# Column sums of a 32768 x 2048 matrix: the last 8-row load shared by two engines, and a first load of 8 rows for each of 48 partitions

## The chip, the cores and the metric

The kernel runs on one core of a Trainium2 chip. The metric is the time of one execution on the device, in microseconds (us). The median of three runs of the kernel before is 628.78 us (628.78 to 629.19). A separate execution was taken with the hardware profiler; every duration below comes from it.

The core has a matrix engine (TensorE, in the profile PE), a vector engine (VectorE, DVE), a scalar engine (ScalarE, ACT), GpSimd (POOL) and SyncE (SP), which here only issues transfers. 16 DMA engines move data between the chip's memory (HBM) and the on-chip memory (SBUF), which has 128 partitions. TensorE writes its sums to PSUM.

## What is computed

```python
def setup_inputs():
    batch, seq, dim = 32, 1024, 2048
    return {
        "grad_output": np.random.randn(batch, seq, dim).astype(np.float32),
    }

def reference(grad_output: np.ndarray) -> np.ndarray:
    return np.sum(grad_output, axis=(0, 1)).astype(np.float32)
```

The input is 32768 rows of 2048 float32 values, 268 MB; the output is one row of 2048 sums. The order of the rows does not matter.

## The kernel before, in words

The matrix is read as a flat list of 32768 rows, that is 256 rows for each of 128 partitions. A load of "m rows" takes 128 x m neighbouring rows and gives each partition m of them, which are contiguous in HBM, so that one partition's piece is m x 8 KB. All loads are issued by SP, in the order of the list `loads`, each with the semaphore that it waits for before it is issued (`after`) and the one that it raises by 16 on landing (`lane`).

The SBUF tile `ring` has three slots (`SLOTS`) of 8 rows (`TILE`) for each partition. The loads, in order:

- `head`, 1 row, into a tile of its own (L84)
- 30 blocks of 8 rows, block k into slot k mod 3 (L85 to L87). From block 3 on, load k waits until the semaphore `vec` has reached k-2, which is the first VectorE add of block k-2. That add is the last reader of the slot which block k overwrites.
- 5 rows into slot 0 (L90), after the first add of block 28; 4 rows into slot 1 (L92), after that of block 29; four loads of 1 row (L93, L94), each after TensorE has used the row which it overwrites (`used`)
- the last two rows, each cut into a left part of 1536 columns and a right part of 512, first both left parts, then both right parts (L99 to L105)

VectorE reduces each block. The first add of block k adds the 4 rows (`WIDE`) left by block k-1 to the first 4 rows of block k, and raises `vec`; the second adds rows 4 to 7 of the block to rows 0 to 3 (L143 to L146, in a loop of 9 passes of 3 blocks). `settle()` drains VectorE between adds that depend on each other. Blocks 28 and 29 and the load of 4 rows are folded to one row by smaller adds, which are ordered by a semaphore `step` (L150 to L173).

TensorE sums over the partitions. A matmul with a column of ones adds one row of each partition into PSUM; the 2048 columns are cut into six pieces, four in LEFT (1536 columns) and two in RIGHT (512), and each piece is two matmul instructions. So a row costs 12. It takes the 5 rows, the four rows loaded one by one, the row that VectorE leaves, and the two last rows in halves (L197 to L209). In the loop of the single rows it also runs filler matmuls of 256 columns whose result nobody reads (L202).

At the end ScalarE and VectorE copy the sums from PSUM to SBUF, left columns first (L219 to L224), and SP writes them out in two transfers (L225 to L228).

Of the kernel before, what the change touches and what calls it, by code (L numbers as in the profile page):

```python
# [8 lines left out]
P = 128  # L9
# [4 lines left out]

SLOTS = 3
TILE = 8
TILES = 30
WIDE = 4
LANES = 4
SMALL = 4  # L20
LAST = 2


LOOPS = 9
ROUNDS = 2

FILLER = 256

LEFT = ((0, 416, 0), (416, 416, 1), (832, 352, 2), (1184, 352, 3))
RIGHT = ((1536, 256, 2), (1792, 256, 3))  # L30
# [3 lines left out]
def kernel(  # L34
# [5 lines left out]
    nc = tc.nc  # L40
    fp32 = mybir.dt.float32
    D = out.shape[-1]
    flat = grad_output.rearrange("b s d -> (b s) d")
    R = flat.shape[0]
    assert (1 + TILE * TILES + 1 + LANES * ROUNDS + SMALL + LAST) * P == R
    assert TILES == SLOTS * (LOOPS + 1)

    const_pool = ctx.enter_context(tc.tile_pool(name="const", bufs=1))
    psum_pool = ctx.enter_context(tc.tile_pool(name="psum", bufs=1, space=bass.MemoryType.PSUM))

    ring = const_pool.tile([P, SLOTS * TILE * D], fp32)
    head = const_pool.tile([P, D], fp32)
    ones = const_pool.tile([P, 1], fp32)
    warm = const_pool.tile([1, 1], fp32)
    psum = psum_pool.tile([P, 3 * 512], fp32)

    names = ("one", "zero", "vec", "step", "used", "mm_left", "mm_right", "done")  # L60
    one, zero, vec, step, used, mm_left, mm_right, done = (tc.alloc_semaphore(n) for n in names)
    slot_in = [tc.alloc_semaphore(f"slot{s}") for s in range(SLOTS)]
    row_in = [tc.alloc_semaphore(f"row{j}") for j in range(LANES)]
    rows_in, small_in = tc.alloc_semaphore("rows"), tc.alloc_semaphore("small")
    last_in = [tc.alloc_semaphore(f"last{i}") for i in range(2 * LAST)]
    left = [tc.alloc_semaphore(f"left{i}") for i in range(2)]
    right = [tc.alloc_semaphore(f"right{i}") for i in range(2)]
    head_in = tc.alloc_semaphore("head")

    def rows(at, m):  # L70
        return ring[:, at * D : (at + m) * D]

    at_row = 0
    loads = []

    def load(m, dst, lane, after=None, first=None, lo=0, hi=D):
        nonlocal at_row
        if first is None:
            first = at_row
            at_row += P * m  # L80
        src = flat[first : first + P * m].rearrange("(p m) d -> p m d", p=P)[:, :, lo:hi]
        loads.append((dst.rearrange("p (m d) -> p m d", m=m), src, lane, after))

    load(1, head[:], head_in)  # L84
    for k in range(TILES):  # L85
        s = k % SLOTS
        load(TILE, rows(s * TILE, TILE), slot_in[s], (vec, k - 2) if k >= SLOTS else None)  # L87


    load(1 + LANES, rows(0, 1 + LANES), rows_in, (vec, TILES - 2))  # L90
    small_at = TILE
    load(SMALL, rows(small_at, SMALL), small_in, (vec, TILES - 1))  # L92
    for j in range(LANES):  # L93
        load(1, rows(j, 1), row_in[j], (used, j + 1))  # L94
    at = (small_at + SMALL) * D
    res_at = at + LAST * D
    final = []
    cut = RIGHT[0][0]
    for lo, hi, pieces in ((0, cut, LEFT), (cut, D, RIGHT)):  # L99
        for j in range(LAST):  # L100
            n = hi - lo
            lane = last_in[len(final)]
            load(1, ring[:, at : at + n], lane, (vec, TILES - 1), at_row + j * P, lo, hi)
            final.append((at, lo, pieces, lane, j == LAST - 1))
            at += n  # L105

# [6 lines left out]
    def take(engine, lane):  # L113
        engine.wait_ge(lane, 16).then_inc(lane, -16)  # L114

    def settle():
        nc.vector.drain(fusable=False)

    def vadd(at, other, n):
        return nc.vector.tensor_add(out=rows(at, n), in0=rows(at, n), in1=other)  # L120

    section = tc.tile_critical(no_gpsimd_drain=True)
    section.__enter__()  # L123
# [2 lines left out]

    nc.gpsimd.memset(ones[:], 1.0).then_inc(one, 1)  # L127

    for lane in row_in:
        nc.gpsimd.wait_ge(rows_in, 16).then_inc(lane, 16)  # L130


    nc.vector.memset(psum[:, : 2 * 512], 0.0).then_inc(zero, 1)  # L133
    take(nc.vector, slot_in[0])
    vadd(0, rows(WIDE, WIDE), WIDE)
    nc.vector.wait_ge(head_in, 16)
    settle()
    vadd(0, head[:], 1)
    with nc.vector.Fori(0, LOOPS):
        for s in (1, 2, 0):  # L140
            at, before = s * TILE, (s - 1) % SLOTS * TILE
            take(nc.vector, slot_in[s])
            settle()  # L143
            vadd(at, rows(before, WIDE), WIDE).then_inc(vec, 1)
            settle()
            vadd(at, rows(at + WIDE, WIDE), WIDE)  # L146
    n_step = 0
    settle()

    def fold(at, height, to, after=None):  # L150
        nonlocal n_step
        while height > to:
            n = min(height // 2, height - to)
            height -= n
            add = vadd(at, rows(at + height, n), n).then_inc(step, 1)
            if after is not None:
                add._wait_ge(*after)
            n_step += 1
            after = (step, n_step)

    height = WIDE
    for k, to in ((TILES - 2, 2), (TILES - 1, 1)):
        at, before = k % SLOTS * TILE, (k - 1) % SLOTS * TILE
        take(nc.vector, slot_in[k % SLOTS])
        add = vadd(at, rows(before, height), height).then_inc(vec, 1)
        if n_step:
            add._wait_ge(step, n_step)
        fold(at, TILE, to, (vec, k))
        height = to
    nc.vector.wait_ge(small_in, 16)  # L170
    fold(small_at, SMALL, 1)
    vadd(at, rows(small_at, 1), 1)._wait_ge(step, n_step).then_inc(step, 1)
    n_step += 1  # L173

# [5 lines left out]
    def matmuls(at, pieces, base=0, wait=None, start=False, then=None):  # L182
        for lo, n, g in pieces:
            x = at + lo - base
            mat = nc.tensor.matmul(  # L185
                sums[lo], lhsT=ones[:], rhs=ring[:, x : x + n], start=start, stop=then is not None
            )
            if wait is not None:
                mat._wait_ge(*wait)
                wait = None  # L190
            if then is not None:
                mat.then_inc(then, 1)
        return mat

    nc.tensor.wait_ge(one, 1)
    nc.tensor.wait_ge(zero, 1)
    matmuls(LANES * D, LEFT + RIGHT, wait=(rows_in, 16), start=True)  # L197
    with nc.tensor.Fori(0, ROUNDS):
        for j, lane in enumerate(row_in):
            take(nc.tensor, lane)  # L200
            if FILLER:
                nc.tensor.matmul(  # L202
                    psum[96:97, 2 * 512 : 2 * 512 + FILLER], lhsT=ones[:], rhs=rows(j, 1)[:, :FILLER], start=True, stop=True
                )
            matmuls(j * D, LEFT + RIGHT).then_inc(used, 1)
    matmuls(at * D, LEFT + RIGHT, wait=(step, n_step))
    for x, lo, pieces, lane, stop in final:
        then = (mm_left if pieces is LEFT else mm_right) if stop else None
        matmuls(x, pieces, lo, wait=(lane, 16), then=then)  # L209


    nc.scalar.copy(out=warm[:], in_=ones[0:1, :])._wait_ge(one, 1)  # L212
# [6 lines left out]
    for copy, half in ((nc.scalar.copy, 0), (nc.vector.tensor_copy, 1)):  # L219
        for i in range(2):  # L220
            lo, n, _ = LEFT[2 * half + i]
            result(copy, lo, n, (mm_left, len(LEFT)), left[half])
        lo, n, _ = RIGHT[half]
# [39 lines left out]
```

## Time and profile before

| Quantity | Before |
|---|---|
| median of 3 runs | 628.78 us |
| the profiled execution | 628.72 us |
| its span (first to last instruction of the program) | 626.9 us |
| VectorE busy | 533.2 us (85%) |
| TensorE busy (matmuls) | 18.8 us (3%) |
| idle time of VectorE ahead of its adds | 84.8 us |
| idle time of TensorE ahead of its first matmul | 598.5 us |
| granted TensorE clock | 0.999 |

A start or an end in the timeline is counted from the beginning of the span. "Idle before" of a group is the time in which the engine did nothing just before its instructions, and the name behind the arrow is what ended most of it: "DVEq L114" is VectorE's own queue standing at the wait of L114 for a block to land. A DMA's time counts from its issue to its landing, so that a transfer which queues behind another seems long. The line of the adds is always L120, that of the helper `vadd`, and that of the matmuls L185.

### The profile page before, as it was taken

To read this page: it belongs to the slowest core of one execution; us is meant where nothing else is said; L and a number is where in the kernel's file an instruction comes from. 1 tells how busy PE (TensorE), PEld (TensorE's weight loads), DVE (VectorE), ACT (ScalarE), POOL (GpSimd) and SP (SyncE) were. 2 spreads that over 40 slices of the span, in tenths; PEclk is the share of its full clock that TensorE was granted. 3 is DMA by queue.
4 is the path that set the end of the run, shared out by engine and by line. 5 is a ranking of instruction groups with operands and counts; after the bars stand their busy time and mean duration, and the time that the engine had idled before them with its cause. 6 is when DMAs were issued, how large, how long until landed. Compare 5 with 4: busy or idle time off the path is not lost. (4 is left out here: it accounts for less than half of the span.)

```text
span 626.9 us, 628 instructions
## 1 busy us (share of the span) xinstructions
PE 18.8 (3%) x160; PEld 6.9 (1%) x160; DVE 533.2 (85%) x70; ACT 2.8 (0%) x5; POOL 0.3 (0%) x5
## 2 busy tenths in 40 slices
PE   0000000000000000000000000000000000000056
PEld 0000000000000000000000000000000000000022
DVE  0349988889888898888988889988889888898995
ACT  0000000000000000000000000000000000000000
POOL 0000000000000000000000000000000000000000
PEclk9999999999999999999999999999999999999999
DMA  9999999999999999999999999999999999999997
GB/s 401 401 468 401 468 401 468 401 468 401 468 401 464 406 456 414 447 422 427 443 427 443 422 447 410 460 406 464 401 468 401 468 401 468 401 468 401 427 415 297
DMA packets 5909, 268.46 MB, mean 428 GB/s; under 512 B 658, under 2 KB 658, under 8 KB 1172
## 3 DMA queue, kind: packets, MB, share of 16 engines
q1 hardware_dynamic: 5908, 268.45, 99.1%
q8 instruction: 1, 0.02, 0.0%
HBM read 268.44 MB, written 0.01 MB: 428 GB/s over the span
## 5 line engine op out<-in xcount | busy, mean ns | idle before, releaser
L120 DVE TENSOR_TENSOR ring<-ring 128x8192 f32<-128x8192 f32 (+2 forms) x65 | 528.6, 8134 | 84.8 <-DVEq L114 82.0
L185 PE MATMUL psum<-ring,ones 128*1 128x352 f32 (+2 forms) x144 | 18.8, 496 | 598.9 <-DMA ring<-in_grad_output_dram 598.9
L185 PEld LDWEIGHTS psum<-ring,ones 128*1 128x1 f32 x144 | 6.5, 86 | 607.6 <-DMA ring<-in_grad_output_dram 600.7
L216 DVE COPY ring<-psum 1x352 f32<-1x352 f32 (+1 forms) x3 | 1.4, 486 | 5.1 <-PE psum L185 5.0
L202 PE MATMUL psum<-ring,ones 128*1 128x256 f32 x16 | 5.2, 410 | 6.1 <-PEq L114 6.1
L216 ACT COPY ring<-psum 1x416 f32<-1x416 f32 (+1 forms) x3 | 1.4, 453 | 620.6 <-PE psum L185 620.5
L120 DVE TENSOR_TENSOR ring<-ring,head 128x2048 f32<-128x2048 f32 x1 | 2.3, 2293 | 0.1
L133 DVE MEMSET psum<- 128x1024 f32 x1 | 0.9, 912 | 1.2 <-SPq L123 1.2
L202 PEld LDWEIGHTS psum<-ring,ones 128*1 128x1 f32 x16 | 1.2, 88 | 8.7 <-issue 8.0
L212 ACT ACT_TABLE_LOAD x1 | 1.3, 1283 | 0.9 <-SPq L123 0.9
L212 ACT COPY warm<-ones 1x1 f32<-1x1 f32 x1 | 0.2, 190 | 0.0
L247 POOL MEMSET const-bfloat16-1.0<- 128x1 bf16 x1 | 0.1, 102 | 0.0
L247 POOL MEMSET const-uint8-127<- 128x1 uint8 x1 | 0.1, 102 | 0.0
L127 POOL MEMSET ones<- 128x1 f32 x1 | 0.1, 100 | 0.5 <-SPq L123 0.5
L247 POOL MEMSET const-float32-0.0<- 128x1 f32 x1 | 0.1, 99 | 0.2 <-issue 0.2
L247 POOL MEMSET const-float32-1.0<- 128x1 f32 x1 | 0.1, 99 | 0.0
## 6 DMA issues: line engine op xcount, KB each, us to landing
ring<-in_grad_output_dram SPq DMA_DIRECT2D x1, 5120.0 KB, 22.6
ring<-in_grad_output_dram SPq DMA_DIRECT2D x1, 4096.0 KB, 14.7
ring<-in_grad_output_dram SPq DMA_DIRECT2D x4, 1024.0 KB, 9.2
ring<-in_grad_output_dram SPq DMA_DIRECT2D x2, 768.0 KB, 13.0
head<-in_grad_output_dram SPq DMA_DIRECT2D x1, 1024.0 KB, 4.9
ring<-in_grad_output_dram SPq DMA_DIRECT2D x2, 256.0 KB, 14.0
ring<-in_grad_output_dram SPq DMA_DIRECT2D x30, 29.8
out_dram<-ring SPq DMA_DIRECT2D x1, 6.0 KB
```

The costliest lines, as they stand in the source:

```text
L120: return nc.vector.tensor_add(out=rows(at, n), in0=rows(at, n), in1=other)
L127: nc.gpsimd.memset(ones[:], 1.0).then_inc(one, 1)
L133: nc.vector.memset(psum[:, : 2 * 512], 0.0).then_inc(zero, 1)
L185: mat = nc.tensor.matmul(sums[lo], lhsT=ones[:], rhs=ring[:, x : x + n], start=start, stop=then is not None)
L202: nc.tensor.matmul(psum[96:97, 2 * 512 : 2 * 512 + FILLER], lhsT=ones[:], rhs=rows(j, 1)[:, :FILLER], start=True, stop=True)
L212: nc.scalar.copy(out=warm[:], in_=ones[0:1, :])._wait_ge(one, 1)
L216: copy(out=res[:, lo : lo + n], in_=sums[lo])._wait_ge(*wait).then_inc(then, 1)
L247: nc = _bacc.Bacc("TRN2", target_bir_lowering=False, num_devices=1)
```

## The change

- `WIDE` goes from 4 to 2. VectorE's part of a block becomes three adds: 2 rows of the block before into this block, then 4 rows, then 2 rows. `vec` is raised by the first of them, as before.
- The first load is no longer 1 row for each of 128 partitions, but 8 rows for each of 48 partitions (`FEW`), the partitions 0 to 47, into slot 2 of the ring. VectorE folds it to 2 rows on 48 partitions and adds these to block 0. Load 2, which overwrites slot 2, now waits for that add. `vec` is one higher than before for the same block, and the gates stand at k-1 instead of k-2.
- The loads of 5, 4 and four times 1 row are gone. In their place come a load of 8 rows into slot 0 (`share_in`), and loads of 2 and 1 rows (`REST`); the last two rows are split as before.
- Of the shared load TensorE takes rows 0 to 2 directly (`DIRECT`). VectorE adds rows 3 to 7 and the sum of everything before (row 8) into row 3, first the left 1536 columns, then the right 512, and raises `sum_left` and `sum_right`. TensorE takes the left sum ahead of the first left part, and the right sum after it, ahead of the second left part.
- The filler matmuls, their loop on TensorE, GpSimd's four waits and the semaphores of the single rows go.

The core of the diff:

```diff
-WIDE = 4
-LANES = 4
-SMALL = 4
+FEW = 48
+WIDE = 2
+DIRECT = 3
+REST = (2, 1)
...
-    load(1, head[:], head_in)
+    head_at = 2 * TILE
+    load(TILE, rows(head_at, TILE)[:FEW], head_in, parts=FEW)
     for k in range(TILES):
         s = k % SLOTS
-        load(TILE, rows(s * TILE, TILE), slot_in[s], (vec, k - 2) if k >= SLOTS else None)
-
-
-    load(1 + LANES, rows(0, 1 + LANES), rows_in, (vec, TILES - 2))
-    small_at = TILE
-    load(SMALL, rows(small_at, SMALL), small_in, (vec, TILES - 1))
-    for j in range(LANES):
-        load(1, rows(j, 1), row_in[j], (used, j + 1))
-    at = (small_at + SMALL) * D
+        load(TILE, rows(s * TILE, TILE), slot_in[s], (vec, k - 1) if k >= 2 else None)
+
+    load(TILE, rows(0, TILE), share_in, (vec, TILES - 1))
+    sum_at = TILE
+    at = sum_at + 1
+    rest = []
+    for m, lane in zip(REST, rest_in):
+        load(m, rows(at, m), lane, (vec, TILES))
+        rest.append((at, m, lane))
+        at += m
+    at *= D
...
-            load(1, ring[:, at : at + n], lane, (vec, TILES - 1), at_row + j * P, lo, hi)
+            load(1, ring[:, at : at + n], lane, (vec, TILES), at_row + j * P, lo, hi)
...
+    nc.vector.wait_ge(head_in, 16)
+    fold(head_at, TILE, WIDE, FEW)
     take(nc.vector, slot_in[0])
-    vadd(0, rows(WIDE, WIDE), WIDE)
-    nc.vector.wait_ge(head_in, 16)
-    settle()
-    vadd(0, head[:], 1)
+    add = vadd(0, rows(head_at, WIDE), WIDE, parts=FEW).then_inc(vec, 1)
+    add._wait_ge(step, n_step)
+    nc.vector.wait_ge(vec, 1)
+    fold(0, TILE, WIDE)
+    nc.vector.wait_ge(step, n_step)
     with nc.vector.Fori(0, LOOPS):
         for s in (1, 2, 0):
             at, before = s * TILE, (s - 1) % SLOTS * TILE
             take(nc.vector, slot_in[s])
             settle()
             vadd(at, rows(before, WIDE), WIDE).then_inc(vec, 1)
-            settle()
-            vadd(at, rows(at + WIDE, WIDE), WIDE)
+            n = TILE
+            while n > WIDE:
+                n //= 2
+                settle()
+                vadd(at, rows(at + n, n), n)
...
+    nc.vector.wait_ge(share_in, 16)
+    for lo, hi, ready in ((0, cut, sum_left), (cut, D, sum_right)):
+        n = TILE - DIRECT + 1
+        while n > 1:
+            m = n // 2
+            x = grid[:, DIRECT : DIRECT + m, lo:hi]
+            add = nc.vector.tensor_add(out=x, in0=x, in1=grid[:, DIRECT + n - m : DIRECT + n, lo:hi])
+            n -= m
+            add._wait_ge(step, n_step)
+            if n > 1:
+                add.then_inc(step, 1)
+                n_step += 1
+            else:
+                add.then_inc(ready, 1)
...
-    matmuls(LANES * D, LEFT + RIGHT, wait=(rows_in, 16), start=True)
-    with nc.tensor.Fori(0, ROUNDS):
-        for j, lane in enumerate(row_in):
-            take(nc.tensor, lane)
-            if FILLER:
-                nc.tensor.matmul(
-                    psum[96:97, 2 * 512 : 2 * 512 + FILLER], lhsT=ones[:], rhs=rows(j, 1)[:, :FILLER], start=True, stop=True
-                )
-            matmuls(j * D, LEFT + RIGHT).then_inc(used, 1)
-    matmuls(at * D, LEFT + RIGHT, wait=(step, n_step))
-    for x, lo, pieces, lane, stop in final:
+    for i in range(DIRECT):
+        matmuls(i * D, LEFT + RIGHT, wait=None if i else (share_in, 16), start=i == 0)
+    for at, m, lane in rest:
+        for i in range(m):
+            matmuls((at + i) * D, LEFT + RIGHT, wait=None if i else (lane, 16))
+    matmuls(DIRECT * D, LEFT, wait=(sum_left, 1))
+    for i, (x, lo, pieces, lane, stop) in enumerate(final):
         then = (mm_left if pieces is LEFT else mm_right) if stop else None
         matmuls(x, pieces, lo, wait=(lane, 16), then=then)
+        if i == 0:
+            matmuls(DIRECT * D, RIGHT, wait=(sum_right, 1))
```

More of the change, by code (lines that the diff above doesn't have):

```diff
@@ L16 @@
 TILE = 8
+FEW = 48
 TILES = 30
-WIDE = 4
-LANES = 4
-SMALL = 4
+WIDE = 2
+DIRECT = 3
+REST = (2, 1)
 LAST = 2
 LOOPS = 9
-ROUNDS = 2
-FILLER = 256
 LEFT = ((0, 416, 0), (416, 416, 1), (832, 352, 2), (1184, 352, 3))
@@ L44 @@
     R = flat.shape[0]
-    assert (1 + TILE * TILES + 1 + LANES * ROUNDS + SMALL + LAST) * P == R
+    assert FEW * TILE + (TILE * TILES + TILE + sum(REST) + LAST) * P == R
     assert TILES == SLOTS * (LOOPS + 1)
@@ L51 @@
     ring = const_pool.tile([P, SLOTS * TILE * D], fp32)
-    head = const_pool.tile([P, D], fp32)
     ones = const_pool.tile([P, 1], fp32)
     warm = const_pool.tile([1, 1], fp32)
[L55 to L65, printed above, removed]
+    psum = psum_pool.tile([P, 2 * 512], fp32)
+    names = ("one", "zero", "vec", "step", "sum_left", "sum_right", "mm_left", "mm_right", "done")
+    one, zero, vec, step, sum_left, sum_right, mm_left, mm_right, done = (tc.alloc_semaphore(n) for n in names)
     left = [tc.alloc_semaphore(f"left{i}") for i in range(2)]
     right = [tc.alloc_semaphore(f"right{i}") for i in range(2)]
-    head_in = tc.alloc_semaphore("head")
+    head_in, share_in = tc.alloc_semaphore("head"), tc.alloc_semaphore("share")
+    slot_in = [tc.alloc_semaphore(f"slot{s}") for s in range(SLOTS)]
+    rest_in = [tc.alloc_semaphore(f"rest{i}") for i in range(len(REST))]
+    last_in = [tc.alloc_semaphore(f"last{i}") for i in range(2 * LAST)]
+    grid = ring.rearrange("p (m d) -> p m d", d=D)
     def rows(at, m):
@@ L74, with load @@
     loads = []
-    def load(m, dst, lane, after=None, first=None, lo=0, hi=D):
+    def load(m, dst, lane, after=None, first=None, lo=0, hi=D, parts=P):
         nonlocal at_row
@@ L79, in load @@
             first = at_row
-            at_row += P * m
-        src = flat[first : first + P * m].rearrange("(p m) d -> p m d", p=P)[:, :, lo:hi]
+            at_row += parts * m
+        src = flat[first : first + parts * m].rearrange("(p m) d -> p m d", p=parts)[:, :, lo:hi]
         loads.append((dst.rearrange("p (m d) -> p m d", m=m), src, lane, after))
-    load(1, head[:], head_in)
+    head_at = 2 * TILE
+    load(TILE, rows(head_at, TILE)[:FEW], head_in, parts=FEW)
     for k in range(TILES):
         s = k % SLOTS
-        load(TILE, rows(s * TILE, TILE), slot_in[s], (vec, k - 2) if k >= SLOTS else None)
-    load(1 + LANES, rows(0, 1 + LANES), rows_in, (vec, TILES - 2))
-    small_at = TILE
-    load(SMALL, rows(small_at, SMALL), small_in, (vec, TILES - 1))
-    for j in range(LANES):
-        load(1, rows(j, 1), row_in[j], (used, j + 1))
-    at = (small_at + SMALL) * D
+        load(TILE, rows(s * TILE, TILE), slot_in[s], (vec, k - 1) if k >= 2 else None)
[8 more added lines that the diff above has]
+    at *= D
     res_at = at + LAST * D
@@ L117, in settle, with vadd @@
         nc.vector.drain(fusable=False)
-    def vadd(at, other, n):
-        return nc.vector.tensor_add(out=rows(at, n), in0=rows(at, n), in1=other)
+    def vadd(at, other, n, to=None, parts=P):
+        out = rows(at if to is None else to, n)
+        return nc.vector.tensor_add(out=out[:parts], in0=rows(at, n)[:parts], in1=other[:parts])
     section = tc.tile_critical(no_gpsimd_drain=True)
@@ L127, with stepped, fold @@
     nc.gpsimd.memset(ones[:], 1.0).then_inc(one, 1)
-    for lane in row_in:
-        nc.gpsimd.wait_ge(rows_in, 16).then_inc(lane, 16)
-    nc.vector.memset(psum[:, : 2 * 512], 0.0).then_inc(zero, 1)
-    take(nc.vector, slot_in[0])
-    vadd(0, rows(WIDE, WIDE), WIDE)
-    nc.vector.wait_ge(head_in, 16)
-    settle()
-    vadd(0, head[:], 1)
+    n_step = 0
+    def stepped(add):
+        nonlocal n_step
+        if n_step:
+            add._wait_ge(step, n_step)
+        add.then_inc(step, 1)
+        n_step += 1
+    nc.vector.memset(psum[:], 0.0).then_inc(zero, 1)
+    def fold(at, n, to, parts=P):
+        while n > to:
+            n //= 2
+            stepped(vadd(at, rows(at + n, n), n, parts=parts))
+    nc.vector.wait_ge(head_in, 16)
+    fold(head_at, TILE, WIDE, FEW)
+    take(nc.vector, slot_in[0])
+    add = vadd(0, rows(head_at, WIDE), WIDE, parts=FEW).then_inc(vec, 1)
[3 more added lines that the diff above has]
+    nc.vector.wait_ge(step, n_step)
     with nc.vector.Fori(0, LOOPS):
@@ L144 @@
             vadd(at, rows(before, WIDE), WIDE).then_inc(vec, 1)
-            settle()
-            vadd(at, rows(at + WIDE, WIDE), WIDE)
-    n_step = 0
-    settle()
[L150 to L159, printed above, removed]
+            n = TILE
+            while n > WIDE:
+                n //= 2
+                settle()
+                vadd(at, rows(at + n, n), n)
+    settle()
     height = WIDE
-    for k, to in ((TILES - 2, 2), (TILES - 1, 1)):
-        at, before = k % SLOTS * TILE, (k - 1) % SLOTS * TILE
-        take(nc.vector, slot_in[k % SLOTS])
+    for k in range(SLOTS * LOOPS + 1, TILES):
+        s = k % SLOTS
+        at, before = s * TILE, (s - 1) % SLOTS * TILE
+        nc.vector.wait_ge(slot_in[s], 16)
         add = vadd(at, rows(before, height), height).then_inc(vec, 1)
@@ L167 @@
             add._wait_ge(step, n_step)
[L168 to L173, printed above, removed]
+        n = TILE
+        while n > 1:
+            n //= 2
+            add = vadd(at, rows(at + n, n), n, sum_at if k == TILES - 1 and n == 1 else None)
+            if n == TILE // 2:
+                add._wait_ge(vec, k + 1).then_inc(step, 1)
+                n_step += 1
+            else:
+                stepped(add)
+        height = 1
+    nc.vector.wait_ge(share_in, 16)
+    for lo, hi, ready in ((0, cut, sum_left), (cut, D, sum_right)):
+        n = TILE - DIRECT + 1
+        while n > 1:
+            m = n // 2
+            x = grid[:, DIRECT : DIRECT + m, lo:hi]
+            add = nc.vector.tensor_add(out=x, in0=x, in1=grid[:, DIRECT + n - m : DIRECT + n, lo:hi])
+            n -= m
+            add._wait_ge(step, n_step)
+            if n > 1:
+                add.then_inc(step, 1)
+                n_step += 1
+            else:
+                add.then_inc(ready, 1)
     sums = {}
@@ L192, in matmuls @@
                 mat.then_inc(then, 1)
-        return mat
     nc.tensor.wait_ge(one, 1)
     nc.tensor.wait_ge(zero, 1)
-    matmuls(LANES * D, LEFT + RIGHT, wait=(rows_in, 16), start=True)
-    with nc.tensor.Fori(0, ROUNDS):
-        for j, lane in enumerate(row_in):
-            take(nc.tensor, lane)
-            if FILLER:
-                nc.tensor.matmul(
-                    psum[96:97, 2 * 512 : 2 * 512 + FILLER], lhsT=ones[:], rhs=rows(j, 1)[:, :FILLER], start=True, stop=True
-                )
-            matmuls(j * D, LEFT + RIGHT).then_inc(used, 1)
-    matmuls(at * D, LEFT + RIGHT, wait=(step, n_step))
-    for x, lo, pieces, lane, stop in final:
+    for i in range(DIRECT):
[5 more added lines that the diff above has]
+    for i, (x, lo, pieces, lane, stop) in enumerate(final):
         then = (mm_left if pieces is LEFT else mm_right) if stop else None
         matmuls(x, pieces, lo, wait=(lane, 16), then=then)
+        if i == 0:
+            matmuls(DIRECT * D, RIGHT, wait=(sum_right, 1))
     nc.scalar.copy(out=warm[:], in_=ones[0:1, :])._wait_ge(one, 1)
```

## The prediction, made before the changed kernel was run

> **What bounds the kernel now.** I read the page first, then the groups of instructions, the timeline of the first blocks and of the last 30 us, and the chain of waits. The page:
>
> ```profile
> span 626.9 us, 628 instructions
> DVE  0349988889888898888988889988889888898995
> DMA  9999999999999999999999999999999999999997
> HBM read 268.44 MB, written 0.01 MB: 428 GB/s over the span
> q1 hardware_dynamic: 5908, 268.45, 99.1%
> ```
>
> The 16 DMA engines are busy in every slice; VectorE, second busiest, always has some idle time. The timeline gives the pace, because each block's first add starts when the block has landed:
>
> ```profile
> 44.67 17.47 DVE L120 TENSOR_TENSOR ring<-ring 128x8192 f32<-128x8192 f32 x2 [8.35 <-DVEq L114]
> ...
> 567.07 50.84 DVE L120 TENSOR_TENSOR ring<-ring 128x8192 f32<-128x8192 f32 x10 [1.82 <-DVEq L114]
> ```
>
> These are blocks 1 and 28. 27 periods in 522.40 us are 19.35 us for 8.39 MB: 433.6 GB/s, or 27.1 GB/s for each of 16 engines. One row for each of 128 partitions (1 MiB, a "row load" below) therefore costs 2.42 us; 256 of them are 619 of the 626.9 us. What is left is about 2 us of start and 3.7 us after the last landing. The end:
>
> ```profile
> 615.70 0.11 PEld L202 LDWEIGHTS psum<-ring,ones 128*1 128x1 f32 x2 [1.35 <-issue]
> 618.19 0.11 PEld L202 LDWEIGHTS psum<-ring,ones 128*1 128x1 f32 x2 [1.36 <-issue]
> 621.91 0.10 PEld L185 LDWEIGHTS psum<-ring,ones 128*1 128x1 f32 x8 [1.13 <-DMA ring<-in_grad_output_dram]
> 622.58 0.09 PEld L185 LDWEIGHTS psum<-ring,ones 128*1 128x1 f32 x4 [0.57 <-DMA ring<-in_grad_output_dram]
> 622.93 1.41 ACT L216 COPY ring<-psum 1x416 f32<-1x416 f32 x3 [620.55 <-PE psum L185]
> 623.20 0.09 PEld L185 LDWEIGHTS psum<-ring,ones 128*1 128x1 f32 x4 [0.53 <-DMA ring<-in_grad_output_dram]
> 624.47 0.25 SPq L228 DMA_DIRECT2D out_dram<-ring  x1
> ```
>
> A row load landed at 615.70, the next at 618.19 (2.49 us for 8 KB pieces); then both left halves by 621.91 (3.72 us), the right halves at 622.58 and 623.20 (0.67, 0.62). TensorE takes each at once. The left sums are ready 1.02 us after the last left half, before the last right half lands: the DMA queue sets the end to the last byte, and no engine is behind it.
>
> VectorE durations for what follows:
>
> ```profile
> L120 DVE TENSOR_TENSOR ring<-ring 128x8192 f32<-128x8192 f32 x58 | 504.2, 8692 | 84.5 <-DVEq L114 82.0
> L120 DVE TENSOR_TENSOR ring<-ring 128x4096 f32<-128x4096 f32 x4 | 17.7, 4423 | 0.1
> L120 DVE TENSOR_TENSOR ring<-ring 128x2048 f32<-128x2048 f32 x3 | 6.9, 2292 | 0.1
> ```
>
> A straight line: 1.042 ns an element plus 0.16 us.
>
> [...] the 256-wide matmul took 634 ns up to 602.3 us, 3.9 us after TensorE's first real work, and 379 ns after.
>
> **The first load (adds the most).** The bytes are the same: head 1 row load, 30 blocks of 8, 5+4+4 and 2 before; 3, 31 blocks of 8, 2+1 and 2 after; 256 each. But the new first load puts 8 rows on partitions 0 to 47 only. [...] not the 3 x 2.42 = 7.26 us of an even spread: 12.1 us late. Nothing gives that back: [...] a block counts as landed only when its slowest part is there. [...] I take 12.1.
>
> **The gates.** Load k still waits for the first add of block k-2. That add is now 2 rows high (4.42 us, not 8.69), so loads are issued 4.3 us earlier; but the queue already holds a whole block then (99.1% busy), so this is worth nothing. Load 2 now waits too, for the head's addition to block 0; block 1, 19.35 us long, is queued meanwhile and covers it. SP is in order, but all its loads have this same order of need. VectorE's block costs 4.42+8.69+4.42 = 17.5 us and about 0.2 us of gaps (before 17.4), under 19.35. Block 28 has four adds, 4.42+8.69+4.42+2.29 = 19.8 us, some 0.7 over, and block 29's 2.29+8.69+4.42+2.29 = 17.7 leave VectorE free about 0.7 us before the shared load lands: nothing. Were that cover gone, each us would lengthen the tail by one. Head folding (8.69+4.42 = 13.1 us) lies in front of block 0's landing.
>
> **Small pieces.** A row load in 8 KB pieces costs 2.49 against 2.42. Before has five, after one and a half: -0.2 us.
>
> **The end.** Let S be the landing of the shared load, last block of 8. Behind it come 2 rows (+4.87), 1 row (+7.36), left halves (+9.22, +11.08), right halves (+11.75, +12.37). VectorE starts at S+0.13 (its usual start) on rows 3 to 7 and the running sum. Left: 4608, 1536, 1536 elements: 4.96+1.76+1.76 us and two gaps of 0.03, done at S+8.67. Right: 1536, 512, 512: 1.76+0.69+0.69 and three gaps, done at S+11.9. TensorE's order is direct rows, 2 rows, 1 row, left sum, left half 0, **right sum**, left half 1, right halves. Its own work is in time: three direct rows, cold at first, to about S+5.2; rows of 1.25 us to S+8.8; left sum and half 0 to S+10.7. Then it waits for the right sum until S+11.9, though left half 1 landed at S+11.08. The right sum's four matmuls take 0.5 us, the last left half 1.02: left copies start at S+13.4, which is 1.05 us after the last landing, where before they started 0.27 us ahead of it (622.93 against 623.20). **+1.3 us**. Not shown before: adds on three separate rows of 1536 or 512. If each row costs nothing extra, +1.3; at 0.16 us a row restart, left and right come 0.6 us later: +1.9; if the last landing is later relative to S by 0.5 us, +0.8. [...] I take warm, as it has the same 3.9 us of unbroken work at S.
>
> **Sum.** The profiled execution took 628.72 us, 1.8 outside its span, and the median is 628.78, 0.06 apart. 628.72 + 12.1 - 0.2 + 1.3 = 641.9; against the median **642.0 us**, span about 640.
>
> **Rivals.**
> - [...] the 48-partition load is 3 row loads, evenly dealt over 16 engines, 7.26 us. Place: the first 10 us. For it: the bytes per engine are equal[...]. Then 628.78 - 0.2 + 1.3 = 629.9, within 0.2% and so not slower. It holds if the first load lands by about 11 us; each us later is a us on the end.
> - *Strided deal* (0.10). If engine e gets partitions e, e+16, e+32, [...] 21.8 late, 651.7 us. [...]
> - *Partly made up or worse* (0.09). [...] 632 to 639.5. [...] over 652.
> [...]
>
> **How the numbers follow.** [...] With the strided deal and a third of the partial cases, 637 to 652 holds 0.81. A measurement of this kernel tells about 0.2% (1.3 us) from no change. [...] all else is slower: 0.02, 0.08, 0.90.
>
> **What would show it.** First block's add: 25.26 us before; about 38 to 40 with the collision, 48 with the strided deal[...]. Period of blocks 1 to 28 unchanged at 19.35. DMA rate in the first two slices well under 400 GB/s. At the end TensorE waits for VectorE (right sum) and the copies start about 1 us after the last landing. The prediction is wrong if block 0 lands by 31 us, if the period moves by over 0.05 us, or if the last right half lands before 634 us.

## The result, and the profile after

The changed kernel takes 647.28 us (median of 5 runs, 646.77 to 647.56) against 628.78 us in the same session. The ratio is 1.0292, with a 95% interval of 1.0278 to 1.0306: 18.5 us slower.

The page of the changed kernel, the lines that answer to those shown of before:

```profile
span 645.1 us, 566 instructions
DVE  0269888889888889888889888889888889888997
DMA  9999999999999999999999999999999999999996
GB/s 130 256 394 455 451 394 455 451 394 455 451 394 455 451 394 455 451 394 455 451 394 455 451 394 455 451 394 455 451 394 455 451 394 455 451 394 455 451 391 265
HBM read 268.44 MB, written 0.01 MB: 416 GB/s over the span
q1 hardware_dynamic: 5396, 268.45, 99.0%
```

The row of GB/s of the kernel before, which the prediction does not show:

```profile
GB/s 401 401 468 401 468 401 468 401 468 401 468 401 464 406 456 414 447 422 427 443 427 443 422 447 410 460 406 464 401 468 401 468 401 468 401 468 401 427 415 297
```

The row of busy shares still shows 9 in every slice but the last, as before. The row of GB/s tells more: the first two slices, 32 us together, run at 130 and 256; the others, up to the last two, at the old pace. So the slices with 130 and 256 GB/s read 9 like the rest: an engine that is held up in a transfer counts as busy.

The start of block 0 in the timeline of the kernel before, then the changed kernel's blocks 0 to 2 and block 28:

```profile
25.26 8.69 DVE L120 TENSOR_TENSOR ring<-ring 128x8192 f32<-128x8192 f32 x1 [23.11 <-DVEq L114]
```

```profile
28.38 13.14 DVE L122 TENSOR_TENSOR ring<-ring 48x8192 f32<-48x8192 f32 x2 [26.23 <-DMA ring<-in_grad_output_dram]
47.61 17.68 DVE L122 TENSOR_TENSOR ring<-ring 48x4096 f32<-48x4096 f32 x3 [6.09 <-DVEq L115]
67.00 17.71 DVE L122 TENSOR_TENSOR ring<-ring 128x4096 f32<-128x4096 f32 x3 [1.71 <-DVEq L115]
86.36 17.71 DVE L122 TENSOR_TENSOR ring<-ring 128x4096 f32<-128x4096 f32 x3 [1.65 <-DVEq L115]
...
589.40 37.78 DVE L122 TENSOR_TENSOR ring<-ring 128x4096 f32<-128x4096 f32 x8 [1.56 <-DMA ring<-in_grad_output_dram]
```

The first load has landed by 28.38, block 0 by 47.61, and from block 1 to block 28 (67.00 to 589.40) 27 periods take 522.40 us again: 19.35 us each, as before. VectorE waits about 1.65 us for each block. Block 0 is 22.35 us later than before; two more row loads ahead of it account for 4.84 of that. So some 17.5 us are lost ahead of 28 us, and neither the lower `WIDE` nor the earlier gates changed the pace.

The windows of the start (DMA share and GB/s are the last two columns; between the length of the window and PEclk stands what PE, PEld, DVE, ACT and POOL were busy):

```profile
0.00:5.00 5.00, 0.00 (x0) 0.00 (x0) 0.91 (x1) 1.47 (x2) 0.30 (x5) 1.00 1.45 210
5.00:10.00 5.00, 0.00 (x0) 0.00 (x0) 0.00 (x0) 0.00 (x0) 0.00 (x0) 1.00 1.47 184
10.00:15.00 5.00, 0.00 (x0) 0.00 (x0) 0.00 (x0) 0.00 (x0) 0.00 (x0) 1.00 0.21 26
15.00:20.00 5.00, 0.00 (x0) 0.00 (x0) 0.00 (x0) 0.00 (x0) 0.00 (x0) 1.00 1.66 210
20.00:25.00 5.00, 0.00 (x0) 0.00 (x0) 0.00 (x0) 0.00 (x0) 0.00 (x0) 1.00 0.00 0
25.00:30.00 5.00, 0.00 (x0) 0.00 (x0) 1.62 (x1) 0.00 (x0) 0.00 (x0) 1.00 1.16 406
```

These bytes are counted where a piece starts, hence the 26 and the 0 in between. ("Piece" is one partition's part of a load, as the list of DMA packets of the trace has it.) The five stretches up to 25 us sum to 630 GB/s x 5 us = 3.15 MB, which is the first load and nothing else. The list shows it as three waves of 16 pieces of 64 KB, that start at 1.95 to 3.29, 8.47 to 11.13 and 16.79 to 19.47 us; in the second and third wave **every** piece takes 8.05 to 8.61 us, where a 64 KB piece of the later blocks takes 2.42.

The end, from the timeline:

```profile
628.04 7.12 PE L212 MATMUL psum<-ring,ones 128*1 128x416 f32 x60 [628.04 <-DMA ring<-in_grad_output_dram]
628.09 11.66 DVE L193 TENSOR_TENSOR ring<-ring 128x4608 f32<-128x4608 f32 x6 [0.91 <-DMA ring<-in_grad_output_dram]
...
639.81 2.06 PE L212 MATMUL psum<-ring,ones 128*1 128x256 f32 x20 [1.55 <-DVE ring L193]
641.07 1.40 ACT L240 COPY ring<-psum 1x416 f32<-1x416 f32 x3 [638.69 <-PE psum L212]
...
642.60 0.26 SPq L252 DMA_DIRECT2D out_dram<-ring  x1
```

The shared load has landed at 628.00 (S in the prediction). VectorE's six adds fill 11.66 us, and TensorE stands 1.55 us for the right sum (`<-DVE ring L193`) until 639.81, though the second left half landed at 639.16. The left copies start at 641.07; the last byte landed at 640.44. Before, the copies were ahead of the last byte.

### The profile page after: what moved, and what is told of

Read it like the earlier page. It is cut to its first block, busy times and chain, and to the rows that moved or that the text cites. A ratio compares the mean times of both kernels' runs of the same rounds, so it can differ in the third digit from the quotient of the medians.

```text
span 645.1 us, 566 instructions
## 1 busy us (share of the span) xinstructions
PE 11.9 (2%) x108; PEld 3.7 (1%) x108; DVE 555.7 (86%) x104; ACT 2.8 (0%) x5; POOL 0.3 (0%) x5
## 5 line engine op out<-in xcount | busy, mean ns | idle before, releaser
L122 DVE TENSOR_TENSOR ring<-ring 128x4096 f32<-128x4096 f32 (+4 forms) x94 | 541.8, 5764 | 83.2 <-DVEq L115 50.5
L212 PE MATMUL psum<-ring,ones 128*1 128x416 f32 (+2 forms) x108 | 11.9, 526 | 629.9 <-DMA ring<-in_grad_output_dram 628.3
L193 DVE TENSOR_TENSOR ring<-ring 128x1536 f32<-128x1536 f32 (+2 forms) x6 | 11.5, 1934 | 1.0 <-DMA ring<-in_grad_output_dram 0.9
L212 PEld LDWEIGHTS psum<-ring,ones 128*1 128x1 f32 x108 | 3.7, 92 | 637.6 <-DMA ring<-in_grad_output_dram 629.7
```

Source lines behind the costliest of these rows:

```text
L122: return nc.vector.tensor_add(out=out[:parts], in0=rows(at, n)[:parts], in1=other[:parts])
L193: add = nc.vector.tensor_add(out=x, in0=x, in1=grid[:, DIRECT + n - m : DIRECT + n, lo:hi])
L212: mat = nc.tensor.matmul(sums[lo], lhsT=ones[:], rhs=ring[:, x : x + n], start=start, stop=then is not None)
```

## The experiments

Each ran on one chip beside the kernel before, which took 628.74 to 628.79 us in all of them. Behind a measured time stand its ratio to the kernel before and the 95% interval of that ratio.

**An even first load, all else as in the changed kernel.** This splits the 18.5 us into the first load and the rest.

```diff
-FEW = 48
+FEW = 128
+HEAD = 3
...
-    load(TILE, rows(head_at, TILE)[:FEW], head_in, parts=FEW)
+    load(HEAD, rows(head_at, HEAD)[:FEW], head_in, parts=FEW)
...
```

> The changed kernel with its first load dealt evenly: 3 rows for each of all 128 partitions, the same 384 rows and bytes. Theory A (the 48 partitions cost the time [...] 25 us instead of 7.3): the first load lands by about 10.5 us, block 0's first add starts near 30, the last landing is near 623.0, and what is left of the change is the late right sum: 629.9 us (+1.1). Rival B (the first load is slow because it is the first and in 64 KB pieces, or because of the new gates): the pieces are 24 KB here, so part of the 17 us stays, 635 or more. Rival C (the tail makes most of the 18.5 us): 640 or more.

Measured: 630.14 us, ratio 1.0022 (1.0014 to 1.0030). Its start in the timeline and in the windows:

```profile
30.68 17.68 DVE L123 TENSOR_TENSOR ring<-ring 128x4096 f32<-128x4096 f32 x3 [17.15 <-DVEq L116]
50.08 13.21 DVE L123 TENSOR_TENSOR ring<-ring 128x4096 f32<-128x4096 f32 x2 [1.71 <-DVEq L116]
```

```profile
0.00:5.00 5.00, 0.00 (x0) 0.00 (x0) 0.91 (x1) 1.47 (x2) 0.30 (x5) 1.00 0.66 221
5.00:10.00 5.00, 0.00 (x0) 0.00 (x0) 0.00 (x0) 0.00 (x0) 0.00 (x0) 1.00 1.07 460
10.00:15.00 5.00, 0.00 (x0) 0.00 (x0) 2.29 (x1) 0.00 (x0) 0.00 (x0) 1.00 1.18 511
```

Block 0's first add starts at 30.68 and not at 47.61. So 17.1 us of the 18.5 (647.28 less 630.14) are the shape of the first load, and 1.4 us (630.14 less 628.74) all the rest. Rivals B and C fall.

**The same bytes on 96 and on 64 partitions.** `FEW`, `HEAD` = 96, 4 and 64, 6.

> The changed kernel with its first load as 4 rows for each of 96 partitions, the same rows and bytes. Theory A with a strided deal (engine e gets partitions e, e+16, e+32 and so on[...]): six waves of 16 pieces of 32 KB[...], the same as with 48: 647.3 us. Rival D ([...] engines get neighbouring partitions): [...] the time is 631 us. Rival E (the loss goes with the number of partitions left out): between, 633 to 640.

> The changed kernel with its first load as 6 rows for each of 64 partitions, the same rows and bytes. Theory A with a strided deal also for 64: [...] 647.3 us. If 64 partitions are dealt in neighbours (4 to an engine), [...] 635.0 us. Rival D [...] 635.0 us; it is told from the neighbour deal by the run with 96 partitions.

Measured: 637.19 us (1.0134, 1.0118 to 1.0149) and 638.37 us (1.0152, 1.0136 to 1.0167). Neither 647.3 nor 631 or 635: both miss for theory A and rival D. 637.19 lies in the range of rival E, a loss that goes with the number of partitions left out; but the losses against the even run are 7.1 us for 32 left out, 8.2 for 64 and 17.1 for 80, not in proportion, and two runs below leave out the same 80 and differ by 2.8 us. The pieces of 96 partitions took 2.2 to 2.6 us after the first wave (32 KB, 1.21 us at the old pace), those of 64 took 3.83 to 3.85 (48 KB, 1.81 us, the last wave up to 3.98). Both are at about half pace: with 64 all 16 pieces of a wave alike, with 96 nearly so. A strided deal is out for these two: waves of 16 neighbouring partitions cost a factor of 3.8, as a run below shows. Why both are at half pace is not shown.

**One wave in the kernel before.** Its first 128 rows as 8 rows for 16 partitions (`FEW` = 16), in slot 2, with load 2 gated by their use.

```diff
-    load(1, head[:], head_in)
+    head_at = 2 * TILE
+    load(TILE, rows(head_at, TILE)[:FEW], head_in, parts=FEW)
...
```

> The kernel before with its first load of 128 rows as 8 rows for each of 16 partitions (in slot 2, load 2 gated by its use), nothing else changed. Theory A: [...] 8.3 us where 2.4 stood: +5.9, 634.7 us. Rival C or a cause in the gates and the smaller adds, which are not in this kernel: 629 us. Rival B (a first load in 64 KB pieces pays for being first): it has such pieces, so some 10 us or more if that were the cost, 639 and up.

Measured: 635.60 us (1.0108, 1.0092 to 1.0123), +6.9 (5.9 expected); the 16 pieces took 8.0 to 9.4 us. The loss comes without the smaller adds, the shared load and the new tail.

**The same pieces on other partitions.** Three loads of 16 partitions, a wave of 16 pieces each.

```diff
-    load(TILE, rows(head_at, TILE)[:FEW], head_in, parts=FEW)
+    for o, lane in zip((0, 4, 1), heads_in):
+        load(TILE, ring[o : P : 8, head_at * D : (head_at + TILE) * D], lane, parts=16)
...
```

> The changed kernel with the same 48 pieces of 64 KB from the same places in HBM, as three loads of 16 partitions each, one for each engine, but on partitions 0, 8, 16 to 120, then 4, 12 to 124, then 1, 9 to 121. These rows are not added, so 384 rows are missing from the output; VectorE's first block is two adds of 2 rows and one more. [...] Theory A [...] 4.2 us a wave, 12.5 for three, and 629.9 + 12.5 - 7.3 = 635.1 us. Rival B (64 KB pieces at the start, or the HBM side of this region, are slow by themselves): 25 us as before, 647 us. [...]

Measured: 637.33 us (1.0135, 1.0119 to 1.0150), ten less than the changed kernel. Block 0's add starts at 38.15 instead of 47.61:

```profile
38.15 13.35 DVE L124 TENSOR_TENSOR ring<-ring 128x4096 f32<-128x4096 f32 x3 [36.00 <-DVEq L117]
```

Size, number, time and place in HBM of the pieces are those of the changed kernel; the destination moved, and one load became three (which by itself changes nothing, as the run with every third partition below shows). They took 4.94 to 4.96 us in the second and third waves instead of 8.3. So the destination decides (rival B falls for good), and on these partitions the pace is half (4.95 is 2.05 x 2.42), worse than the 4.2 expected.

**Which deal?** The same three loads on 16 neighbouring partitions each, and, with `ring[j : FEW : 3, ...]` in place of the slice, on every third one.

```diff
-    load(TILE, rows(head_at, TILE)[:FEW], head_in, parts=FEW)
+    for j, lane in enumerate(heads_in):
+        load(TILE, ring[16 * j : 16 * j + 16, head_at * D : (head_at + TILE) * D], lane, parts=16)
...
```

> The changed kernel with its first load written out as three loads of 16 neighbouring partitions each (0-15, 16-31, 32-47), 8 rows each, the same pieces to the same partitions, so that each of the 16 engines gets one piece of each load. This is the strided deal by hand. If one 48-partition load is dealt like that, nothing moves: waves of 8.3 us, block 0's first add at 47.6, 647.3 us. If the 48 were dealt in neighbours [...] this is still 8.3 to 8.5 us a wave; so this run is the control for the next one.

> As the run with three loads of 16, but on partitions 0, 3 to 45, then 1, 4 to 46, then 2, 5 to 47: the neighbour deal by hand (engine e gets 3e, 3e+1, 3e+2). [...] If one 48-partition load is dealt strided (my theory), this is faster than it: [...] 16 to 20 us for the three waves and uneven pieces of 2.5 to 7.5 us, 638 to 643 us. If it is dealt in neighbours, this run is the same as the 48-partition load: even pieces of 8.3 us and 647.3 us.

Measured: 649.95 us (1.0338, 1.0322 to 1.0354), with pieces of 9.31 us; and 647.15 us (1.0290, 1.0275 to 1.0306), with pieces of 8.29 to 8.39 us. The second run is the changed kernel to 0.1 us, in time and in its pieces; the first is 2.7 us slower, and its 9.31 us a piece were foreseen by neither branch. My strided theory falls: the load of 48 behaves as if dealt in neighbours, 3e to 3e+2 to engine e (inferred from the two times, as the list of packets names neither the engine nor the partition of a piece). The two runs write the same bytes to the same 48 partitions, so these alone don't set the time either: it counts which 16 are written together. And the second run shows what I had not thought of: no piece of a wave gets ahead, 8.29 to 8.39 us for all, where my theory had uneven ones of 2.5 to 7.5. The start in the timeline of the second run:

```profile
28.71 13.13 DVE L124 TENSOR_TENSOR ring<-ring 48x8192 f32<-48x8192 f32 x2 [26.56 <-DMA ring<-in_grad_output_dram]
47.91 13.22 DVE L124 TENSOR_TENSOR ring<-ring 48x4096 f32<-48x4096 f32 x2 [6.06 <-DVEq L117]
```

28.71 and 47.91, where the changed kernel has 28.38 and 47.61. Put together (pieces after the first wave; the old pace is that of the later blocks, 64 KB in 2.42 us):

| First load | us per piece | at the old pace | factor |
|---|---|---|---|
| 128 x 3 rows | 0.91 | 0.91 | 1.0 |
| 96 x 4 | about 2.4 | 1.21 | 2.0 |
| 64 x 6 | 3.84 | 1.81 | 2.1 |
| 16 at a time, every eighth | 4.95 | 2.42 | 2.0 |
| 48 x 8; 16 at a time, every third | 8.33 | 2.42 | 3.4 |
| 16 at a time, neighbours | 9.31 | 2.42 | 3.8 |

The last three rows move the same 48 pieces, so the factors of 2.0, 3.4 and 3.8 are those of the partitions that are written together. Every load of fewer than 128 partitions that was run has a factor of about 2 or more; what makes one set of partitions slower than another is not shown.

**The tail: TensorE's order.** Even first load, the right sum behind the second left half.

```diff
-        if i == 0:
+        if i == 1:
             matmuls(DIRECT * D, RIGHT, wait=(sum_right, 1))
```

> The changed kernel with the even first load (3 rows for 128 partitions) and TensorE's right sum moved behind the second left half instead of ahead of it. Theory (TensorE waits in its own order for VectorE's right sum while the left half lies there): the left copies start 1.02 us after the last left half again, about 0.3 us ahead of the last landing, and the tail is that of the kernel before: 628.6 us, 1.2 below the even run. Rival (the tail is late because TensorE is cold or VectorE's sums are late in themselves): at most 0.3 below the even run.

Measured: 629.27 us (1.0009, 1.0000 to 1.0017), 0.87 below the even run (1.2 expected):

```profile
623.25 1.45 ACT L243 COPY ring<-psum 1x416 f32<-1x416 f32 x3 [620.86 <-PE psum L215]
```

TensorE's wait for VectorE went, as the theory says: copies start at 623.25, ahead of the last landing at 623.45. What stays is the transfers' own lateness: that last landing was at 623.16 in the kernel before.

**The tail: fewer rows for VectorE.** Even first load, `DIRECT` 4.

> The changed kernel with the even first load and four rows of the shared load taken by TensorE (DIRECT 4), so that VectorE adds 5 rows instead of 6. Same theory from the other side: VectorE's chain is 11.6 us less about 1.7, the right sum is ready near S+10 ahead of the second left half at S+11.1, and TensorE no longer waits: 628.6 us. Rival (the sums' place in TensorE's order costs nothing, the tail is cold matmuls): one more cold row at S, later by about 0.8 us, 630.5 us.

Measured: 630.05 us (1.0020, 1.0011 to 1.0030), no gain: a miss for the theory as I wrote it. But the timeline shows that its mechanism worked and something else ate it:

```profile
623.10 1.01 ACT L243 COPY ring<-psum 1x416 f32<-1x416 f32 x2 [620.71 <-PE psum L215]
...
624.43 0.60 PE L215 MATMUL psum<-ring,ones 128*1 128x256 f32 x4 [1.09 <-DMA ring<-in_grad_output_dram]
```

The left copies start early, at 623.10; then TensorE waits 1.09 us for the last right half. 15 engines had landed it by 623.32, the sixteenth at 624.38. The page has this line in every run, also before:

```profile
q8 instruction: 1, 0.02, 0.0%
```

It is a fetch of 16 KB of instructions, which took 1.07 to 1.09 us in each run. Here it started at 621.81, 1.5 us ahead of the other engines' last landing; before it started at 622.55 and in the even run at 622.64, 0.6 and 0.9 us ahead.

**Is it the fetch?** The run with `DIRECT` 4, less the fourth direct row's 12 matmuls; and, as a version meant to win, the first load of before with 2, 2 and 1 rows behind the shared load, which makes TensorE's program longer.

> The even first load with DIRECT 4 again, but TensorE leaves out the fourth direct row's 12 matmuls (128 rows are missing from the output), so that it has as many instructions as the even run with DIRECT 3. In the DIRECT 4 run the profile has an instruction fetch (16 KB on a DMA queue of its own) at 621.81, ahead of the last landings, and one engine's last landing came 1.1 us after the others; in the other runs the fetch came at 622.6. Theory: TensorE's 24 more instructions bring the fetch forward into the last transfers, which costs its 1.09 us on one engine. Then here it is back at 622.6, the last right half lands by 623.5, and the time is 628.9 us. Rival (DIRECT 4 is late for another reason, its sums): 630.05 again.

> The changed kernel with the first load of before (1 row for each of 128 partitions) and the two row loads so freed behind the shared load (2, 2, 1 rows and the halves). VectorE's right sum at S+11.9 then has until the last left half at S+16, so TensorE no longer waits: the tail of before. By the transfers alone 628.6 us, not slower than before. But TensorE has 24 more instructions written out than the changed kernel; if the instruction fetch theory holds, the fetch falls into the last transfers and costs up to 1.1 us: 629.7.

Measured: 629.26 us (1.0007, 0.9999 to 1.0015) with the fetch at 622.38 and the last landing at 623.54, as in the even run; and 629.92 us (1.0019, 1.0011 to 1.0027) with the fetch at 621.56 and one engine late again:

```profile
623.87 1.23 PE L214 MATMUL psum<-ring,ones 128*1 128x256 f32 x8 [1.10 <-DMA ring<-in_grad_output_dram]
```

Its last two landings came at 623.82 and 624.45, the other fifteen engines' at 622.48 and 623.11 at the latest. With 108 matmuls written out (the even run, this one without the fourth row) the fetch starts at 622.64 and 622.38, with 120 at 621.81, with 132 at 621.56, and the late engine comes and goes with it. In both runs that have it, a piece on that engine starts within 0.02 us of the end of the fetch (622.89 and 622.90, 622.64 and 622.65), and it and the next three take 0.15 to 0.23 us, where all other pieces of that size take 0.08 to 0.10. (629.26 is 0.4 above my number; the last landing was 0.4 later than before, as in the even run.)

**The two put right together.** First load of before, 2, 2 and 1 rows, `DIRECT` 1, right sum last, 108 matmuls.

> The changed kernel with the first load of before (1 row for each of 128 partitions), 2, 2 and 1 rows behind the shared load, only one row of it taken directly by TensorE (DIRECT 1, so VectorE adds 8 rows, left done near S+11.8, right near S+16.2), and the right sum behind the second left half in TensorE's order. TensorE has the 108 matmuls of the changed kernel, 24 fewer than the run with DIRECT 3 and the same loads. If the instruction fetch is then back at 622.4 or later [...]: 628.6 us, the same as before within 0.2. If the fetch still comes ahead of the last transfers[...]: 629.5 to 630.

Measured: 628.80 us against 628.79 (1.0003, 0.9995 to 1.0011). The fetch started at 622.41, the last byte landed at 623.18, the second write-out was issued at 624.52 (before: 623.16, 624.47). With the first load and the tail undone, nothing of the 18.5 us is left. It doesn't beat the kernel before; no version here did.

## Why the prediction was right or wrong

Forecast was 642.0 us, slower, with 637 to 652 as the range; 647.28 came. Direction and range hold; the narrower 640 to 645, to which I had given 0.68 as the likeliest case, does not. That the wide range holds is in part luck: its upper end was there for the strided deal, which is not what happened. By its own signs (block 0 at 38 to 40 us for the forecast, 48 for the strided deal) the measured 47.61 would even have been read as the strided deal; only the deals written out by hand told the two apart.

- **The bound.** Right: the pace of 19.35 us a block is the same, and everything that changed is in when the transfers start running freely and in the tail. (The account of the 626.9 us as 619, 2 and 3.7 leaves some 2 us unexplained; no term of the forecast rests on them.)
- **The first load, +12.1.** Right in that the 48 partitions cost time, too small in its size, and this is the step that failed. 19.35 us for this load (7.26 + 12.1) was my estimate; no trace showed it, as every load of the kernel before writes all 128 partitions. In fact the load is three waves, in the second and third of which every piece takes about 8.3 us, 25.6 us from the first start to the last end (1.95 to 27.52), where the 24 KB pieces of an even one take 8 x 0.91 = 7.3; measured on the whole kernel, 17.1 us more (647.28 - 630.14). Why a piece takes 8.3 us, and so what makes up the 5.0 us missed, is not shown.
- **As fast as three row loads (0.13).** Refuted: the load took 25.6 us, not 7.26. Moving the destination alone changes its pieces (4.95 us against 8.3).
- **Strided deal (0.10).** Written out by hand it gives 649.95 us; the load of 48 isn't it. It had been near in time for a wrong reason, as 16 neighbours at a time cost a factor of 3.8 and the true waves 3.4.
- **The gates and VectorE's blocks, 0.** Right: 1.65 us of waiting are left for each block, and VectorE was free 0.91 us before the shared load (0.7 foreseen).
- **Small pieces, -0.2.** Wrong in sign. In the even run the last byte landed at 623.54, 0.4 later than before. The first wave of pieces runs at about half pace in both (0.58 us for 8 KB, 1.65 us for 24 KB, against 0.31 and 0.91), so larger first pieces would lose more. That fits the other runs, but was not tried by itself: leaving the late engine aside, the last landing is at 623.32 to 623.54 in the four runs with the even first load and at 623.11 to 623.18 in the three with the first load of before.
- **The end, +1.3.** Mechanism right, size 0.9. Left and right sums were ready at S+8.6 and S+11.8 (8.67 and 11.9 foreseen), TensorE was at its faster pace (from 636 us on its 256-wide matmuls took 379 ns), and it waited as described. But the right sum and the last left half took 1.24 us together, queued back to back, where I had added 0.5 and 1.02: copies 0.63 us after the last landing, not 1.05. Undoing the order returned 0.87 us.

Sum of what was measured: 17.1 + 0.4 + 0.9 = 18.4, of 18.5.

## What to carry to other kernels

A transfer on fewer partitions was not priced by its bytes here: against the pace of a load on all 128, 96, 64 and every eighth partition cost a factor of about 2, the partitions 0 to 47 in one load 3.4 and 16 neighbours at a time 3.8. Nor do the partitions alone set it: the same 48 took 8.33 or 9.31 us a piece, by which 16 were written together. In these runs such a first load cost 6.9 us against the kernel before and 7.1 to 19.8 against the even one, so measure its pieces, on just the partitions that are meant, before counting on it. In this kernel, which the transfers bound, the 17 us lost in the first load were never made up; look at the GB/s of the slices and not at the DMA's busy share, which read 9 in the slow slices (130 and 256 GB/s) too. In the last few us, check where the instruction fetch falls before giving TensorE more instructions: with 108 matmuls written out it started at 622.38 to 622.64, with 120 and 132 at 621.81 and 621.56, and there one engine was 1.1 to 1.3 us late.

## What was not expected of the hardware

- The 16 pieces of a wave kept one pace: in the run with every third partition, every piece of the second and third wave took 8.29 to 8.39 us, where a 64 KB piece of the later blocks takes 2.42. Why none gets ahead, and why every eighth partition, every third and neighbours cost 2.0, 3.4 and 3.8, was not tried and stays open.
- A 16 KB instruction fetch of 1.09 us is served among the transfers: started 1.5 us ahead of the other engines' last landing, it went with one engine that was 1.1 to 1.3 us late (two profiles); started 0.6 to 1.2 us ahead, with none (the other twelve). That it was served by that same engine is inferred from the piece that starts as the fetch ends.
